# A two-layer decoder trunk on one core: the first sums of its modulation in pairs, and a new order of issue

## The chip, the cores and the metric

One core of a Trainium2 chip. Its engines work side by side: TensorE (PE, with its weight loads shown apart as PEld), VectorE (DVE), ScalarE (ACT), GpSimd (POOL) and SyncE (SP), which here only issues DMA transfers. Each engine works through its own instructions in the order in which they were issued, and waits on semaphores for the others. The metric is the device time of one execution in microseconds (us).

## The reference

A decoder trunk of two layers on x of 256 tokens by 1024 features, float32 throughout. An even layer is a combined input projection for two groups of heads (a sliding-window attention with sinks, and a sparse one with compressed, selected and window branches); an odd layer is a block-sparse attention that is a causal one at this length. What surrounds each layer is the part that this change touches:

```
c_act = silu(c)
for layer in range(2):
    ada = einsum('bd,de->be', c_act, w_ada[layer]) + b_ada[layer]
    shift, scale, gate = split(ada, 3, axis=-1)
    h = rms_norm(x, norm_g[layer]) * (1 + scale) + shift
    y = even_mixer(h, ...) if layer == 0 else odd_mixer(h, ...)
    x = x + gate * y
return rms_norm(x, final_g)
```

Layer 0 can multiply nothing by its input weights before shift and scale are there for at least a few features, and these need a matrix product of c (one row) with `w_ada`.

## The kernel before

**One list sets the order.** The whole trunk is first recorded: each call on an engine becomes a numbered operation in a `Plan`, with the operations that must come before it. Then `issue` goes through `ORDER`, a list of 3002 numbers, and issues the operations in that order. It demands only that what an operation depends on comes earlier in the list, so the list decides the order on every engine's queue, DMA issues included. All instructions carry line L244, that of the helper, so in the profile they are told apart by the names of their tiles. `group` gives a handful of operations the union of what any of them depends on, so that they stand together behind the same waits.

**The float32 products.** A large operand is split into a float32r part `hi` (a cast on ACT, tiles `whi`) and the rest `lo` (a subtraction on DVE, tiles `wlo`); the activations are split into `hhi` and `hlo`. A product is three matmuls, hi by hi, hi by lo and lo by hi, into the same bank.

**The opening.** The 1024 features are eight blocks of 128. `START` deals them out in four units: two blocks, then two, two and two. For each unit the kernel loads the columns of `w_ada` for that unit's shift and scale (1024 rows by 512 columns, 2 MB), sums them against c, turns the sums into columns (`shs`), prepares `hhi` and `hlo` of the unit's blocks, and multiplies them by the corresponding 128-row blocks of the input weights (`raw`, 128 x 1688 each, loaded in pieces of 1304 and 384 columns or finer), accumulating in the banks `ps_s`, `ps_pj`, `ps_o` and `ps_pt`. Before that come the squares of x, its scaling, and its transposes through `ps_s` and `ps_pj` into `bigA`. PE runs matmuls on `ones` in between, for which no one waits.

Unit 0's columns of `w_ada` go to four rooms: `qT_98` (shift, features 0 to 511 of c), `qT_99` (shift, 512 to 1023), `qT_100` (scale, first half) and `gate` (scale, second half, loaded in two pieces). Unit 2 uses the same rooms again; units 1 and 3 use `late`. `cz` holds silu(c) in column 0 of 32 columns, for each of eight slices k of c.

**The sums** (`start_sums`). For each of four column groups q (0 and 1 are the two blocks of shift, 2 and 3 those of scale) one row of 32 output partitions is used: the matmul has 32 stationary columns (`cz[:, k]`) at tile position 32 q and 128 moving columns. For unit 0 (d = 0) all eight k are summed on PE, 32 matmuls. For later units the first d slices are summed on DVE into `acc` and go in as one extra matmul. In the kernel before, the loops run over k outside and q inside, and groups of four matmuls are tied together. When all is summed, ACT copies the bank to `asb`, PE transposes it, DVE adds the bias and applies the norm's weight.

**The end.** After the output projection of layer 1, for each half of the tokens, DVE adds the scaled result to `xs`, sums squares, POOL takes the root, and ACT and DVE scale the columns and send them out in pieces (`LAST`): of the first half 384 columns by ACT and 640 by DVE; of the second half 192 and 192 by ACT, 256 and 384 by DVE. In the profile the scaled results are tiles `t`, and `parts` holds the sums of squares.

**Small rows.** `rows` collects norm weights, biases and the compressed branch's position terms, each a load of 16 rows of 128 (8 KB), for layer 1 and the compressed branch among them.

Of the kernel before, what the change touches and what calls it, by code (L numbers as in the profile page):

```python
# [255 lines left out]
def tile_trunk(  # L256
# [23 lines left out]
    plan = Plan(tc.nc)  # L280
# [433 lines left out]
    def start_sums(g, n, d, w):  # L714
# [29 lines left out]
        for o in range(0, len(ids), 4):  # L744
            plan.group(ids[o : o + 4])
# [640 lines left out]
```

## Time and profile before

| what | value |
|---|---|
| median of 3 runs | 295.09 us (294.73 to 295.18) |
| the profiled execution's own time | 295.04 us |
| its span, first to last instruction | 293.3 us |
| mean granted clock of TensorE | 0.995 |
| PE, DVE, ACT busy | 285.4, 252.8, 188.5 us |
| bytes moved by DMA | 71.72 MB |

The span is what the rows of the trace count from; 1.74 us of the execution's time lie around it. A busy engine is not one that works at its peak: PE's matmuls overlap and their ends are modelled. The granted clock was 1.00 in nearly all stretches, so it plays no part here. In rows of the timeline the first number is the start in us, the second the length of the group; a bracket at the end is the idle time ahead of it and what ended it. Rows of the chain of waits give start, length, and what the end of the program was waiting for at that time.

### The profile page before, as it was taken

What the parts mean: (1) busy time and instruction counts of PE and PEld (TensorE: products, weight loads), DVE (VectorE), ACT (ScalarE), POOL (GpSimd) and SP (SyncE); (2) the same over time, 40 slices, a digit from 0 to 9 for tenths busy, and PEclk for the clock granted to TensorE, in tenths of its full rate; (3) what the DMA queues carried; (4) which work ended last, traced back from release to release, by engine and by line L of the source; (5) the groups of instructions that cost most, each with busy time, mean ns of one, the idle gap of its engine ahead of it and who ended that gap; (6) DMA issues with size and microseconds to landing.
All of it is one profiled execution on the core that took longest, in us unless ns stands there. A gap on an engine that the chain in (4) does not pass through costs nothing.

```text
span 293.3 us, 6197 instructions
## 1 busy us (share of the span) xinstructions
PE 285.4 (97%) x2293; PEld 246.6 (84%) x2293; DVE 252.8 (86%) x629; ACT 188.5 (64%) x480; POOL 8.1 (3%) x33
## 2 busy tenths in 40 slices
PE   8999999999999999999999999999999999999991
PEld 8888788897897888777767899998899999887891
DVE  0497797999999999999889759779978999899884
ACT  4456256895998899994457863366658368584531
POOL 3000000000000000000020000000000000000021
PEclk9999999999999999999999999999999999999998
DMA  7999999999969942769986954569489709502003
GB/s 262 381 365 380 384 380 349 344 349 322 389 233 359 351 147 74 249 234 332 333 256 206 349 167 135 191 242 283 146 258 291 244 0 335 205 36 72 1 3 142
DMA packets 48431, 71.72 MB, mean 245 GB/s; under 512 B 2490, under 2 KB 33938, under 8 KB 48402
## 3 DMA queue, kind: packets, MB, share of 16 engines
q1 hardware_dynamic: 47906, 70.93, 70.6%
q8 instruction: 18, 0.29, 0.4%
q10 hardware_dynamic: 496, 0.41, 0.4%
q14 instruction: 11, 0.09, 0.1%
HBM read 70.28 MB, written 1.05 MB: 243 GB/s over the span
## 4 chain that ended last, share of the span: by engine, by line
PE 82%; DMA 11%; DVE 1%; ACT 1%; issue 1%; POOL 1%; POOLq 0%; DVEq 0%; ACTq 0%
PE ps_pj L244 53%; PE ps_s L244 10%; PE ps_o L244 7%; PE ps_pt L244 7%; PE ps_m L244 5%; DMA gate<-in_w_ada_dram 3%; DMA late<-in_w_ada_dram 3%; DMA raw<-in_w_in_even_dram 3%; DMA qT<-in_w_ada_dram 2%; DMA xs<-in_x_dram 1%; DVE wlo L244 1%; ACT t L244 1%; ACT whi L244 1%; POOL parts L244 1%; DVE t L244 0%
## 5 line engine op out<-in xcount | busy, mean ns | idle before, releaser
L244 ACT CAST whi<-raw 128x512 fp32r<-128x512 f32 (+2 forms) x116 | 71.8, 658 | 27.1 <-PE ps_pj L244 16.5
L244 DVE TENSOR_TENSOR wlo<-raw,whi 128x512 fp32r<-128x512 f32 (+2 forms) x100 | 71.3, 740 | 7.3 <-ACT whi L244 6.6
L244 PE MATMUL ps_pj<-hlo,whi 128*128 128x256 f32 x256 | 70.0, 288 | 0.0
L244 PE MATMUL ps_pj<-hhi,whi 128*128 128x256 f32 x256 | 69.9, 289 | 0.0
L244 PE MATMUL ps_pj<-hhi,wlo 128*128 128x256 f32 x256 | 68.3, 284 | 0.0
L244 PEld LDWEIGHTS ps_pj<-hhi,whi 128*128 128x128 f32 x256 | 46.7, 188 | 1.6 <-issue 0.7
L244 PEld LDWEIGHTS ps_pj<-hlo,whi 128*128 128x128 f32 x256 | 47.1, 189 | 0.8 <-issue 0.7
L244 PEld LDWEIGHTS ps_pj<-hhi,wlo 128*128 128x128 f32 x256 | 46.7, 189 | 0.3
L244 ACT ACTIVATE late<-late,mn 128x128 f32<-128x128 f32 (+1 forms) x58 | 26.0, 450 | 9.2 <-DVE mn L244 9.1
L244 DVE SCALAR_TENSOR_TENSOR acc<-raw,cz,acc 128x1024 f32<-128x1024 f32 x24 | 30.6, 1276 | 0.1
L244 PE MATMUL ps_pj<-whi,hlo 128*128 128x512 f32 (+2 forms) x72 | 25.6, 373 | 0.0
L244 PE MATMUL ps_pj<-wlo,hhi 128*128 128x512 f32 (+2 forms) x72 | 25.5, 372 | 0.0
L244 DVE SCALAR_TENSOR_TENSOR wlo<-raw,whi 128x512 fp32r<-128x512 f32 x32 | 21.1, 686 | 4.5 <-ACT whi L244 4.4
L244 PE MATMUL ps_pj<-whi,hhi 128*128 128x512 f32 (+2 forms) x72 | 24.8, 373 | 0.0
L244 PE MATMUL ps_pj<-wlo,ghi 128*128 128x512 f32 (+1 forms) x56 | 20.6, 371 | 0.0
L244 PE MATMUL ps_pj<-whi,ghi 128*128 128x512 f32 (+1 forms) x56 | 20.6, 371 | 0.0
L244 PE MATMUL ps_pj<-whi,glo 128*128 128x512 f32 (+1 forms) x56 | 20.4, 367 | 0.0
L244 PE MATMUL ps_pt<-ta,late 128*128 128x128 f32 x87 | 19.6, 275 | 0.0
L244 ACT COPY late<-ps_pt 128x384 f32<-128x384 f32 (+1 forms) x29 | 14.0, 483 | 7.9 <-PE ps_pt L244 7.6
L244 PEld LDWEIGHTS ps_pj<-whi,hhi 128*128 128x128 f32 x72 | 13.4, 188 | 2.5 <-ACT hhi L244 0.7
L244 PEld LDWEIGHTS ps_pj<-whi,hlo 128*128 128x128 f32 x72 | 13.6, 188 | 2.0 <-issue 0.2
L244 PEld LDWEIGHTS ps_pj<-wlo,hhi 128*128 128x128 f32 x72 | 13.4, 189 | 1.6
(243 smaller groups left out, 591.0 us busy)
## 6 DMA issues: line engine op xcount, KB each, us to landing
raw<-in_w_in_odd_dram SPq DMA_DIRECT2D x16, 1024.0 KB, 5.7
raw<-in_w_ada_dram SPq DMA_DIRECT2D x8, 1024.0 KB, 8.3
raw<-in_w_ada_dram SPq DMA_DIRECT2D x16, 512.0 KB, 6.3
raw<-in_w_in_even_dram SPq DMA_DIRECT2D x5, 1024.0 KB, 7.9
raw<-in_w_in_even_dram SPq DMA_DIRECT2D x7, 652.0 KB, 7.6
late<-in_w_ada_dram SPq DMA_DIRECT2D x16, 256.0 KB, 6.8
raw<-in_w_out_even_dram SPq DMA_DIRECT2D x4, 1024.0 KB, 5.8
raw<-in_w_out_odd_dram SPq DMA_DIRECT2D x4, 1024.0 KB, 8.7
```

The lines of the kernel that those rows point to most:

```text
L244: self.ops.append(dict(key=eng.key, deps=deps, fn=lambda: getattr(real, name)(*args, **kw)))
```

## The change

In `start_sums` the matmuls of unit 0 are recorded in pairs: first q = 0 and 1 (shift) for all k, then q = 2 and 3 (scale) for all k, and two rather than four are tied together. Units 1 to 3 are recorded as before. The second part is a new `ORDER`. The operations are the same and so is their number.

```
-        for m in range(max(len(tq) for tq in terms)):
-            for q, tq in enumerate(terms):
-                if m < len(tq):
+        size = 4 if d else 2
+        for o in range(0, 4, size):
+            for m in range(max(len(tq) for tq in terms)):
+                for q in range(o, o + size):
+                    tq = terms[q]
+                    if m >= len(tq):
+                        continue
                     ids.append(T.matmul(
...
-        for o in range(0, len(ids), 4):
-            plan.group(ids[o : o + 4])
+        for o in range(0, len(ids), size):
+            plan.group(ids[o : o + size])
...
 ORDER = [int(i) for i in """
-5 0 45 4 9 685 2 3 6 10 37 7 1 85 11 40 38 35 86 12 87 13 14 15 16 17 70 18 88 19 89 20 71 21 72 22 55 23 46 41 39 42 47
...
```

What the order of issue shows, at three places. First PE in the opening, before: the end of unit 0's sums (`ps_m`) up to the first matmul of the projection. Ahead of these rows the same alternation of shift rooms and `qT_100` or `gate` fills twelve rows.

```order
L244 MATMUL ps_m_107<-qT_99,cz 32x128 x2
L244 MATMUL ps_m_107<-gate,cz 32x128 x2
L244 MATMUL ps_m_107<-qT_99,cz 32x128 x2
L244 MATMUL ps_m_107<-gate,cz 32x128 x2
L244 MATMUL ps_s_93<-ta,t_89 128x128
L244 MATMUL ps_pj_95<-ta,t_91 128x128
L244 MATMUL ps_m_107<-ta,asb_108 128x128
L244 MATMUL ps_pj_95<-ta,t_91 128x128
L244 MATMUL ps_o_68<-ones 128x128
L244 MATMUL ps_pj_95<-ta,t_91 128x128
L244 MATMUL ps_o_68<-ones 128x128 x3
L244 MATMUL ps_s_93<-whi_110,hhi 128x512
```

In the changed kernel the shift sums on `qT_98` come right after the transposes of the first x tiles (the words to the right of the arrow are what the matmul reads):

```order
L244 MATMUL ps_o_68<-ones 128x128 x7
L244 MATMUL ps_s_92<-ta,t_89 128x128 x2
L244 MATMUL ps_m_107<-qT_98,cz 32x128 x8
L244 MATMUL ps_pt_85<-ta,rows 128x24
L244 MATMUL ps_s_92<-ta,t_89 128x128
L244 MATMUL ps_pj_94<-ta,t_91 128x128
L244 MATMUL ps_o_68<-ones 128x128
```

and the end of the sums, up to the first matmul of the projection, reads:

```order
L244 MATMUL ps_m_107<-qT_100,cz 32x128 x2
L244 MATMUL ps_s_92<-ta,t_89 128x128
L244 MATMUL ps_s_93<-ta,t_89 128x128
L244 MATMUL ps_m_107<-qT_100,cz 32x128 x2
L244 MATMUL ps_m_107<-gate,cz 32x128 x8
L244 MATMUL ps_s_93<-ta,t_89 128x128 x3
L244 MATMUL ps_pj_95<-ta,t_91 128x128 x2
L244 MATMUL ps_m_107<-ta,asb_108 128x128
L244 MATMUL ps_o_68<-ones 128x128
L244 MATMUL ps_pj_95<-ta,t_91 128x128
L244 MATMUL ps_o_68<-ones 128x128 x4
L244 MATMUL ps_s_92<-whi_110,hhi 128x512
```

All sums on the shift rooms now stand ahead of the last on `qT_100`, the eight matmuls on `gate` stand alone at the end, and five transposes of x stand between them and the transpose of the sums (`asb_108`).

Second, SP's queue in the opening, before: `raw_101` and `raw_102` are the weights of blocks 0 and 1, `late` unit 1's columns of `w_ada`.

```order
L244 DMA gate<-in_w_ada_dram 128x2x256 x2
L244 DMA raw_101<-in_w_in_even_dram 128x512
L244 DMA raw_101<-in_w_in_even_dram 128x792
L244 DMA raw_101<-in_w_in_even_dram 128x384
L244 DMA raw_102<-in_w_in_even_dram 128x1304
L244 DMA late<-in_w_ada_dram 128x2x256 x2
L244 DMA raw_102<-in_w_in_even_dram 128x384
L244 DMA late<-in_w_ada_dram 128x2x256 x6
L244 DMA raw_103<-in_w_in_even_dram 128x1304
L244 DMA raw_103<-in_w_in_even_dram 128x384
```

The same stretch now:

```order
L244 DMA gate<-in_w_ada_dram 128x2x256
L244 DMA rows<-in_b_ada_dram 16x128
L244 DMA gate<-in_w_ada_dram 128x2x256
L244 DMA raw_101<-in_w_in_even_dram 128x512
L244 DMA rows<-in_cmp_pe_v_dram 16x128
L244 DMA raw_101<-in_w_in_even_dram 128x384
L244 DMA raw_101<-in_w_in_even_dram 128x792
L244 DMA raw_102<-in_w_in_even_dram 128x384
L244 DMA qT_100<-in_w_ada_dram 128x2x256
L244 DMA raw_102<-in_w_in_even_dram 128x1304
L244 DMA late<-in_w_ada_dram 128x2x256 x5
L244 DMA rows<-in_cmp_pe_k_dram 16x128
```

Two loads of `rows` that stood far down the queue are here now (a third follows among `late`), and one of the pieces of unit 2's columns (`qT_100`, 256 KB), which stood behind `raw_104`, now precedes the 1304 columns of `raw_102`. Unit 2's other pieces follow where they did, behind `raw_104`, in another order, with both pieces for `gate` last.

Third, DVE at the end of the program, before: `t_89` takes the 640 scaled columns of the first half of the tokens, `t_88` columns of the second half, `ISA` is the sum of squares.

```order
L244 TENSOR_TENSOR xs<-xs,t_91 128x256
L244 TENSOR_TENSOR xs<-xs,bigA 128x512
L244 TENSOR_SCALAR t_89<-xs,parts 128x640
L244 TENSOR_TENSOR xs<-xs,bigA 128x256
L244 TENSOR_TENSOR xs<-xs,bigA 128x512
L244 TENSOR_TENSOR xs<-xs,ps_pj_95 128x256
L244 ISA t_90,parts<-xs,parts 128x256
L244 ISA parts 128x1
L244 TENSOR_SCALAR t_88<-xs,parts 128x384
L244 SCALAR_TENSOR_TENSOR t_88<-xs,parts,bigA 128x256
```

Now:

```order
L244 TENSOR_TENSOR xs<-xs,t_91 128x256
L244 TENSOR_TENSOR xs<-xs,bigA 128x512
L244 TENSOR_TENSOR xs<-xs,bigA 128x256
L244 TENSOR_TENSOR xs<-xs,ps_pj_95 128x256
L244 ISA t_90,parts<-xs,parts 128x256
L244 ISA parts 128x1
L244 TENSOR_SCALAR t_89<-xs,parts 128x640
L244 TENSOR_SCALAR t_88<-xs,parts 128x384
L244 SCALAR_TENSOR_TENSOR t_88<-xs,parts,bigA 128x256
```

The scaling into `t_89` stands behind the last sum of squares, ahead of the two of the second half. The order changed at many other places on all engines too, with the same operations.

231 rows, old and new, of the table ORDER are left out of this document.

## The prediction

> **What bounds the kernel now.** I read the page's busy shares first, then a table of stretches of the span, then the chain of waits. The page:
>
> ```profile
> PE 285.4 (97%) x2293; PEld 246.6 (84%) x2293; DVE 252.8 (86%) x629; ACT 188.5 (64%) x480; POOL 8.1 (3%) x33
> ```
>
> The share is an average. The table of stretches (start and end, length; then busy time and count for PE, PEld, DVE, ACT, POOL; granted clock, DMA share, GB/s) tells the stages apart:
>
> ```profile
> 0.00:15.00 15.00, 13.84 (x136) 12.85 (x137) 4.42 (x16) 6.97 (x14) 3.32 (x21) 1.00 0.92 323
> 15.00:33.00 18.00, 17.50 (x128) 14.50 (x131) 15.61 (x32) 8.98 (x20) 0.00 (x0) 1.00 1.07 373
> 33.00:52.00 19.00, 19.00 (x154) 16.21 (x153) 15.77 (x36) 10.98 (x24) 0.00 (x0) 1.00 1.05 366
> 75.00:105.00 30.00, 30.00 (x264) 25.62 (x264) 29.98 (x105) 26.87 (x86) 0.00 (x0) 1.00 0.90 320
> 167.00:240.00 73.00, 73.00 (x632) 68.54 (x632) 61.93 (x148) 40.88 (x97) 0.00 (x0) 1.00 0.62 205
> 275.00:293.30 18.30, 12.05 (x76) 10.63 (x74) 11.85 (x25) 5.46 (x13) 2.30 (x5) 0.92 0.16 59
> ```
>
> Up to 33 us the DMA engines are full; from 33 to 275 PE has no idle time; at the end PE is idle while the last rows are written. The 13.84 us of PE in the first row hold the warm-up matmuls on `ones` and other work of the opening; the first matmul of a projection comes at 14.74 (a row below). The row of 167 to 240 gives a price: 632 matmuls in 73.00 us is 0.1155 us for 256 columns, so 0.23 for 512. The chain of waits in its first 36 us (start, length, what) says which transfers set the opening:
>
> ```profile
> 0.80 3.35 DMA xs<-in_x_dram
> 4.16 7.62 DMA gate<-in_w_ada_dram
> 11.79 7.51 DMA late<-in_w_ada_dram
> 19.32 7.42 DMA raw<-in_w_in_even_dram
> 26.75 6.09 DMA qT<-in_w_ada_dram
> 32.89 1.30 PE ps_m L244 x40
> 34.19 0.67 PE ps_s L244 x2
> ```
>
> Each link is issued when an earlier transfer has landed: the second half of `gate` lands at 11.78, one transfer of `late` goes out at 11.79. Behind the last link PE takes over. So there are two barriers: the second `gate` for unit 0, and unit 2's sums at 32.89, the only place after the start where PE waited for data:
>
> ```profile
> PE ps_m L244 <- DMA qT<-in_w_ada_dram: 0.5, 1, 0.5
> ```
>
> PE reached them at 32.39. What is won ahead of 32.39 is not kept unless this barrier moves too. This is the centre of the forecast.
>
> **The change part by part.** *Unit 0's sums.* The timeline of before, DVE's row of `cz` first (start, length, what, count; one fp32 matmul on PE leaves two records):
>
> ```profile
> 9.16 0.17 DVE L244 TENSOR_SCALAR cz<-tiny 128x8 f32<-128x8 f32 x1
> 11.05 1.18 PE L244 MATMUL ps_m<-qT,cz 128*32 128x128 f32 x34
> 12.73 0.28 PE L244 MATMUL ps_m<-gate,cz 128*32 128x128 f32 x2
> 13.42 0.33 PE L244 MATMUL ps_m<-ta,asb 128*128 128x128 f32 x1
> 14.74 0.70 PE L244 MATMUL ps_s<-whi,hhi 128*128 128x512 f32 x2
> 32.89 0.64 PE L244 MATMUL ps_m<-qT,cz 128*32 128x128 f32 x16 [0.50 <-DMA qT<-in_w_ada_dram]
> 33.35 0.40 PE L244 MATMUL ps_m<-gate,cz 128*32 128x128 f32 x8
> 33.57 0.40 PE L244 MATMUL ps_m<-acc,ones 128*32 128x128 f32 x8
> 33.79 0.40 PE L244 MATMUL ps_m<-gate,cz 128*32 128x128 f32 x8
> ```
>
> A quad of four sums is 8 records and takes 33.57 - 33.35 = 0.22 us. In before all 8 quads run in one go, 11.05 to 13.01, and only then can the sums be copied and turned. Now the shift pairs, which need only `qT`, run ahead, and four pairs on `gate` are left for the end. No row shows a pair alone. From below it costs half a quad (0.11), from above a whole one (0.22), since the two columns that are missing ran beside the others; I take 0.22. In the new order three places have two pairs of different columns back to back, which I count as quads: 13 steps, 13 x 0.22 = 2.9 against 8 x 0.22 = 1.8, so 1.1 us more of PE. Nearly all of it lies in time in which PE ran `ones` and waited for landings. What counts is behind `gate`'s second half (11.78): two to four pairs, 0.44 to 0.88, so the sums end at 12.3 to 12.7 against 13.0. The earlier `cz` on DVE (the scalings of both halves of x stood ahead of it, now one does) is what lets the shift pairs go first. The first real matmul, 14.74, comes 1.7 us behind the sums by the chain copy, transpose, two small DVE operations, `hhi`, and some of the ACT casts stand beside it: I take 14.4, a gain of 0.3.
>
> The Trainium skill, TensorEngine Tiling (Array Packing), Theoretical Speedup, puts a stationary side of at most 32 at up to four times, by filling four column tiles. By it a pair wastes half the array and sixteen pairs would be 16 x 0.22 = 3.5 us; the quads of this trace, four sums in 0.22, agree with the packing, and no run here shows a pair. It changes the result only if PE and not `gate` ends the sums.
>
> *The opening's transfers.* The old queue, as SP issued it:
>
> ```profile
> 3.31 1.22 SPq L244 DMA_DIRECT2D gate<-in_w_ada_dram  x2
> 4.66 2.95 SPq L244 DMA_DIRECT2D raw<-in_w_in_even_dram  x4
> 8.79 1.89 SPq L244 DMA_DIRECT2D late<-in_w_ada_dram  x2
> 11.05 0.34 SPq L244 DMA_DIRECT2D raw<-in_w_in_even_dram  x1
> 11.79 5.90 SPq L244 DMA_DIRECT2D late<-in_w_ada_dram  x6
> 27.53 0.37 SPq L244 DMA_DIRECT2D gate<-in_w_ada_dram  x1
> ```
>
> Moved ahead: three loads of `rows` of 8 KB each and one 256 KB piece of `qT` that unit 2 needs, now in front of the 652 KB piece of `raw_102`, row block 1 of the input projection. At the 373 GB/s of the stretch 15 to 33 that is 0.7 us for the 256 KB and under 0.1 for all three small ones. So `raw_102` and unit 1's `late` come 0.7 to 0.8 later than before. The `qT` piece overwrites what the scale pairs of k = 0 and 1 read, so SP waits for PE there, with `raw_102` and all of `late` queued behind it; as PE can take those pairs before `gate` is in, I count nothing for it; if they ran last SP would go on at 12.3 instead of about 11 (it issued the other piece of `raw_102` at 11.05), and `raw_102` could come up to 1.3 later still, which B would need. PE starts on row block 1 some 3.5 us behind its first matmul (its place in the new order at the price above); I expect a stall of 0.5 to 1.0 there or at unit 1's sums, which eats the 0.3 and more. But what counts is unit 2's last `gate`: ahead of it lie 10,544 KB of SP's queue before (counted from the order) and 10,568 now, so it lands at most 0.1 later. The real matmuls ahead of unit 2's sums are the same, 15.7 us at the price above in either order. So PE arrives at 32.39 - 0.3 + (0.5 to 1.0) = 32.6 to 33.1, and waits there as before; up to about 33.2 the late arrival costs nothing, because the last 8 records on `gate` at 33.79 end the sums in any case. **Opening: between -0.5** (the barrier's whole idle time gone) **and +0.9; taken 0.**
>
> *The middle.* The same instructions in another order, under a PE that has no idle time: 0, as long as that cover holds. What an order can win or lose there are the weight loads' waits, 34 to 275 us; the largest:
>
> ```profile
> PEld ps_s L244 <- DVE mn L244: 0.8, 1, 0.8
> PEld ps_pj L244 <- ACT hhi L244: 0.7, 2, 0.4
> PEld ps_s L244 <- DVE qT L244: 0.6, 3, 0.3
> ```
>
> These three sum to 2.1 us, and as PE shows no idle time beside them at most part reached the matmuls. I bound the middle at -1.0 (half of them gone) and, by the same size, +1.0: in 75 to 105 DVE was busy 29.98 of 30.00, and a chain that moves there has nothing to hide behind. Taken -0.1, near the no-idle row.
>
> *The tail.* The scaling of 640 columns of the first half of the tokens moves on DVE from ahead of the last sums to behind them. Rows of the tail:
>
> ```profile
> 285.84 0.55 DVE L244 TENSOR_SCALAR t<-xs,parts 128x640 f32<-128x640 f32 x1
> 286.31 1.02 DVE L244 TENSOR_TENSOR xs<-xs,bigA 128x256 f32<-128x256 f32 x2
> 286.43 3.81 SPq L244 DMA_DIRECT2D out_dram<-t  x3
> 286.78 0.27 PE L244 MATMUL ps_pj<-whi,glo 128*128 128x256 f32 x1
> 287.25 0.41 DVE L244 TENSOR_TENSOR xs<-xs,ps_pj 128x256 f32<-128x256 f32 x1
> 288.38 0.55 POOL L244 TENSOR_TENSOR parts<-parts,expo 128x1 f32<-128x1 f32 x1 [1.93 <-DVE parts L244]
> 288.96 0.42 DVE L244 TENSOR_SCALAR t<-xs,parts 128x384 f32<-128x384 f32 x1 [0.67 <-POOL parts L244]
> ```
>
> PE's last matmul is over at 287.05, and DVE began on its result at 287.25, straight behind its own work: at most 0.2 to win, 0.17 taken for the handover. The moved 0.55 now lies in DVE's 0.67 of waiting for POOL, so it costs nothing while POOL takes that long. But its 320 KB of output leave at about 288.7 instead of 286.43, just ahead of the last 512 KB. At 373 GB/s they are 0.9 us; if all of that stood in the way the tail would lose 0.7, if none it would win 0.17. The last transfers go out from 289.4 on, so most is through: I take +0.1 for it, net -0.07.
>
> **Sum** against the profiled execution (span 293.3, its own time 295.04, so 1.74 around the span; the median of the runs is 295.09): 295.04 + 0 - 0.1 - 0.07 = 294.87; I say 294.9.
>
> **The rivals.** *A, faster: the order's gains are kept.* Unit 2's barrier gives back its 0.5, the tail 0.17, and 0.1 to 0.5 of the weight loads' waits goes: 295.04 - 0.8 to - 1.2 = 293.8 to 294.2. For it: the waits are real. Against: the bytes ahead of the barrier have not become fewer.
>
> *B, slower: `raw_102` behind `qT`.* The 652 KB piece lands 0.8 late, PE stalls at row block 1, unit 1's sums come 0.8 late, and both add up instead of falling together. From an arrival at unit 2 beyond 33.2 on each tenth counts; 32.09 + 1.6 = 33.7 gives +0.5, and with the blocked end of the tail (up to 0.7) +0.5 to +1.2: 295.5 to 296.2, about 295.8. For it: the DMA share of 1.07, no slack in the queue. Against: both stalls stem from one delay of 0.7.
>
> *C: small transfers are dear.* Issues wait for earlier landings (11.78, then 11.79), so a load of 8 KB takes a place in the queue like one of 256 KB. If each of the three left a hole of 0.2 the barrier would come 0.6 later: 295.5.
> The Trainium skill, DMA: Bandwidth & Descriptors, Anatomy of one DMA, gives a transfer about 2.0 us of fixed cost (a fit on the software-made kind); in series the three would be an estimated 6 us and the result 301. The chain above, with full DMA engines at seven microseconds from issue to landing, speaks against series; what one small load costs amid large ones no row of before separates.
>
> *D: it does not do what it says.* PE takes the pairs no earlier than the quads, since `cz` is not ready: then they start at 9.33, when `cz` was ready before, and 2.9 us end at 12.2, below 12.7. It falls to the same time.
>
> **How the numbers follow.** About 0.2% (0.59 us) is what a measurement of this kernel can tell from no change. The forecast, 294.5 to 295.5, has 0.47; A 0.28; B 0.15; C 0.06; D lies within the forecast with 0.04. A is faster by over 0.2% but for its edge: with the forecast's low end 0.30. B and C past 295.68: 0.19, with the middle's +1.0. Same: 0.51. The range holds A's upper part, the forecast and B's middle: 294.1 to 295.9; the forecast's own is 294.5 to 295.5.
>
> **What would show it.** Right: first real matmul at 14.3 to 14.5; a DMA wait of `raw` or `whi` at 17 to 19; unit 2's sums still ending at 34.0 to 34.3; PE's last matmul within 0.5 of 286.78; DVE on its result within 0.1 of the matmul's end. Wrong: unit 2's sums ending before 33.7 or after 34.8, or PE idle between 35 and 275.

## The result: 297.71 us against 295.01, slower by 0.9%

| what | before | changed |
|---|---|---|
| median | 295.01 us (294.73 to 295.18, 4 runs) | 297.71 us (296.75 to 297.89, 4 runs) |
| ratio | 1 | 1.0086, 95% interval 1.0063 to 1.0109 |
| the profiled execution's own time | 295.04 us | 297.89 us |
| its span | 293.3 us | 296.1 us |

The prediction was 294.9 with a range of 294.1 to 295.9: wrong in direction and outside the range. The changed kernel's page, first the busy shares and then the table of stretches (start and end, length; busy time and count of PE, PEld, DVE, ACT, POOL; granted clock, DMA share, GB/s):

```profile
PE 287.5 (97%) x2293; PEld 248.1 (84%) x2293; DVE 252.6 (85%) x629; ACT 188.6 (64%) x480; POOL 10.5 (4%) x33
```

```profile
0.00:15.00 15.00, 13.88 (x129) 12.51 (x130) 3.52 (x13) 6.03 (x12) 3.08 (x19) 1.00 0.87 297
15.00:33.00 18.00, 17.54 (x126) 14.50 (x125) 14.82 (x32) 9.95 (x22) 0.00 (x0) 1.00 1.03 345
275.00:296.10 21.10, 14.54 (x87) 12.61 (x85) 15.14 (x30) 7.11 (x16) 4.70 (x5) 0.94 0.14 50
```

PE's share is the same 97%; nothing in the first row speaks of 2.7 us. The GB/s at the end of the stretches do: 297 instead of 323 in the first 15 us, 345 instead of 373 in the next 18. Those are 0.39 and 0.50 MB that had not been moved by then. Two narrow stretches, of the changed kernel and then of the kernel before, show where most of it is missing:

```profile
13.60:16.40 2.80, 2.80 (x26) 2.51 (x23) 1.89 (x6) 2.44 (x7) 0.00 (x0) 1.00 0.62 142
```

```profile
13.60:16.40 2.80, 2.80 (x20) 2.54 (x19) 2.54 (x7) 2.80 (x7) 0.00 (x0) 1.00 1.04 379
```

142 GB/s for 2.80 us instead of 379: 0.66 MB, or 1.75 us of transfers at the old rate. There was a hole in a queue that had none before. SP's queue and its waits between 2 and 20 us tell why (rows of the timeline, then of the table of waits: us in total, times, longest):

```profile
8.00 3.35 SPq L244 DMA_DIRECT2D raw<-in_w_in_even_dram  x3
13.08 0.38 SPq L244 DMA_DIRECT2D qT<-in_w_ada_dram  x1
13.50 1.52 SPq L244 DMA_DIRECT2D raw<-in_w_in_even_dram  x1
15.06 2.87 SPq L244 DMA_DIRECT2D late<-in_w_ada_dram  x5
```

```profile
SPq L244 <- PE ps_m L244: 1.3, 1, 1.3
```

SP had issued three pieces of `raw` by 11.35 and then stood until 13.08 at the moved piece of `qT_100`. Up to then each issue had followed by some 0.02 us the landing of the transfer eight places ahead: 8.00 behind 7.99, 9.51 behind 9.49, 11.02 behind 11.00. The next such landing came at 11.75. From there to 13.08 are the 1.3 us for which the row names PE. On PE:

```profile
8.39 1.07 PE L244 MATMUL ps_m<-qT,cz 128*32 128x128 f32 x16
11.26 1.07 PE L244 MATMUL ps_m<-qT,cz 128*32 128x128 f32 x28
12.26 0.44 PE L244 MATMUL ps_s<-ta,t 128*128 128x128 f32 x2
12.62 0.41 PE L244 MATMUL ps_m<-qT,cz 128*32 128x128 f32 x4
12.87 1.04 PE L244 MATMUL ps_m<-gate,cz 128*32 128x128 f32 x16
15.70 0.70 PE L244 MATMUL ps_s<-whi,hhi 128*128 128x512 f32 x2
```

The piece overwrites what the sums of k = 2 and 3 on `qT_100` read. (The prediction wrote k = 0 and 1; the piece holds columns 512 to 1023 of the room, the third and fourth slice.) The last of these pairs stands behind two transposes of x and runs at 12.62. Behind the piece wait `raw_102` (652 KB) and all of `late`. Worked out from the landings in the trace, `raw_102` is complete at 19.11 instead of 15.52, the last `late` at 25.07 instead of 23.03, and the last `gate` of unit 2 at 35.89 instead of 33.54. The chain of waits now runs through the same places (pieces left out between):

```profile
12.69 0.37 PE ps_m L244 x4
13.06 0.02 issue
13.08 0.38 SPq L244
...
13.50 1.52 SPq L244
...
16.56 5.52 DMA late<-in_w_ada_dram
...
22.10 6.60 DMA raw<-in_w_in_even_dram
...
28.77 7.12 DMA gate<-in_w_ada_dram
...
35.93 0.43 PE ps_m L244 x8
```

PE's pair, SP's issues, then three transfers, each behind the landing of the one before, up to the end of unit 2's sums: 35.93 + 0.43 = 36.36, against 33.79 + 0.40 = 34.19. The barrier moved by 2.2 us. From there PE keeps that lag and adds little: its last matmul starts at 289.27, 2.49 behind the 286.78 of before. The end of the program, in the timeline:

```profile
289.27 0.27 PE L244 MATMUL ps_pj<-whi,glo 128*128 128x256 f32 x1
289.58 0.42 DVE L244 TENSOR_TENSOR xs<-xs,ps_pj 128x256 f32<-128x256 f32 x1 [0.36 <-PE ps_pj L244]
290.56 0.55 DVE L244 TENSOR_SCALAR t<-xs,parts 128x640 f32<-128x640 f32 x1
290.72 0.79 POOL L244 TENSOR_TENSOR parts<-parts,expo 128x1 f32<-128x1 f32 x1 [1.45 <-DVE parts L244]
291.17 1.67 SPq L244 DMA_DIRECT2D out_dram<-t  x3
291.54 0.42 DVE L244 TENSOR_SCALAR t<-xs,parts 128x384 f32<-128x384 f32 x1 [0.44 <-POOL parts L244]
```

DVE is free for PE's result: 0.31 from the last matmul's start to its own, 0.47 before. But POOL's root takes 0.79 beside the moved scaling, 0.55 before, so the last scalings start 2.27 behind PE's last matmul (2.18 before). From there to the end of the span are 4.56 us (4.34 before), with 320 KB more ahead of the last output. Together 0.31 later. So of the span's 2.8 us 2.17 arise up to the end of unit 2's sums, 0.32 between there and PE's last matmul, and 0.31 behind it.

### The profile page after: what moved, and what is told of

The parts are those of the page before. It is cut to its first block, busy times and chain, and to the rows that moved or that the text cites. A ratio compares the mean times of both kernels' runs of the same rounds, so it can differ in the third digit from the quotient of the medians.

```text
span 296.1 us, 6176 instructions
## 1 busy us (share of the span) xinstructions
PE 287.5 (97%) x2293; PEld 248.1 (84%) x2293; DVE 252.6 (85%) x629; ACT 188.6 (64%) x480; POOL 10.5 (4%) x33
## 4 chain that ended last, share of the span: by engine, by line
PE 86%; DMA 6%; DVE 2%; SPq 1%; issue 1%; POOL 0%; POOLq 0%; ACT 0%; DVEq 0%; ACTq 0%
PE ps_pj L244 55%; PE ps_o L244 10%; PE ps_s L244 8%; PE ps_pt L244 7%; PE ps_m L244 6%; DMA gate<-in_w_ada_dram 2%; DMA raw<-in_w_in_even_dram 2%; DMA late<-in_w_ada_dram 2%; DVE t L244 1%; SPq L244 1%; DVE xs L244 1%; POOL parts L244 0%; POOLq L1385 0%; ACT t L244 0%; DVEq L1385 0%
## 5 line engine op out<-in xcount | busy, mean ns | idle before, releaser
L244 PE MATMUL ps_pj<-whi,hhi 128*128 128x512 f32 (+2 forms) x72 | 26.3, 372 | 0.0
L244 PE MATMUL ps_pt<-ta,late 128*128 128x128 f32 x87 | 19.0, 274 | 0.0
L244 ACT COPY asb<-ps_m 128x128 f32<-128x128 f32 (+1 forms) x7 | 2.2, 312 | 19.8 <-PE ps_m L244 19.8
```

Source lines behind the costliest of these rows:

```text
L244: self.ops.append(dict(key=eng.key, deps=deps, fn=lambda: getattr(real, name)(*args, **kw)))
```

## The experiments

In the diffs the numbers are operations in `ORDER`: 216 is the moved piece of `qT_100` (columns 512 to 1023), 215 the other, 211 the first piece of `qT_98`, 101 the 1304 columns of `raw_102`, 102 its 384, 93 to 100 `late`, 526, 528 and 529 small loads of `rows`, 2936 DVE's scaling of 640 columns and 2937 its output. Each median stands beside the kernel before in the same batch, on one chip. The changed kernel itself had medians of 297.71, 296.48 and 297.72 in three batches, so where figures of two batches are put together, the text says so. The ratios go by means and can differ from the quotient of the medians. A profile shows one execution, and where a kernel's runs scatter it can lie well above the median. In some of the kernels the helper stands in line L249.

### First batch: one part of the change undone or done alone

**The `qT` piece back** (changed kernel, 216 to its old neighbours):

```
-... 132 133 216 134 79 ...  248 252 215 193 ...
+... 132 133 134 79 ...  248 252 216 215 193 ...
```

> The changed kernel with one transfer moved: the 256 KB piece of qT for unit 2 goes back behind raw_104, next to the other piece of qT_100. Theory H (a hole in the transfers: SP stood before that piece from 11.4 to 13.07 waiting for PE's last pair on qT_100, and the DMA engines ran dry behind it): SP no longer waits, raw_102's 1304 columns land at 16 to 17.5 instead of 19.1, unit 2's last gate at 33.6 to 34.3 instead of 35.9, and the time falls by 1.5 to 2.3, to 295.4 to 296.2. Theory S (the small loads of rows leave holes) and theory M (the new order behind 36 us is what is slow): at most 0.5 less, 297.2 or more.

Measured: 296.23 us against 295.02 (ratio 1.0041, 1.0029 to 1.0053). SP goes on to `raw_102` at once, and unit 2's sums end at 34.44, 0.25 behind before:

```profile
11.01 1.07 SPq L249 DMA_DIRECT2D raw<-in_w_in_even_dram  x2
34.04 0.40 PE L249 MATMUL ps_m<-gate,cz 128*32 128x128 f32 x8
```

H had given 295.4 to 296.2. The hole comes with the piece. 1.2 us stay, which it does not explain.

**The piece ahead of `raw_102` in the kernel before** (101 and two of `late` follow it):

```
-... 62 52 101 63 ... 67 95 103 ... 112 98 113 ... 117 118 119 ... 199 216 254 ...
+... 62 52 63 ... 67 103 ... 112 113 ... 117 118 216 101 95 98 119 ... 199 254 ...
```

> The kernel before with the opposite move alone: the same 256 KB piece of qT ahead of raw_102's 1304 columns, quads as they were. Theory H: SP waits for the last quad on qT_100, at about 12.0, raw_102 lands 1.5 to 3 later than 15.5, the last gate of unit 2 0.6 to 1.8 later than 33.5, and the time rises by 0.6 to 1.8, to 295.6 to 296.8. Theory S and theory M: no change, within 0.3 of 295.0, since the bytes ahead of the barrier stay the same.

Measured: 296.00 us against 295.02 (1.0046, 1.0027 to 1.0065): about 1.0 slower with this move, within H's 0.6 to 1.8; the three loads had to go behind the piece with it. In the profile (297.16, well above the median) SP waits there too (`SPq <- PE ps_m` 1.1 us), and the sums of unit 2 end 1.8 later:

```profile
12.44 0.38 SPq L249 DMA_DIRECT2D qT<-in_w_ada_dram  x1
35.62 0.40 PE L249 MATMUL ps_m<-gate,cz 128*32 128x128 f32 x8
```

**The three small loads of `rows` back** (rival C of the prediction):

```
-... 88 526 56 ... 23 529 24 ... 149 528 171 ... 409 421 530 ...
+... 88 56 ... 23 24 ... 149 171 ... 409 421 529 528 526 530 ...
```

> The changed kernel with its three small loads of rows (8 KB each) moved back to where they stood, ahead of srow's load. Theory S: 0.6 or more less, 297.1 or below. Theory H: SP's wait at the piece of qT is the same, so at most 0.3 less, 297.4 to 297.9.

Measured: 296.99 us against 295.02 (1.0066, 1.0045 to 1.0086), and the wait is there as before: `qT` goes out at 13.24, with 1.7 us of waiting for PE. The small loads are not the cause of the hole. What they are worth in time is not settled: 296.99 lies below the 297.1 that S had named, but the changed kernel was not in this batch, and its own medians reach from 296.48 to 297.72.

**The tail back** (changed kernel, scaling and output of the 640 columns ahead of the last sums):

```
-... 2963 2978 ... 2992 2936 2993 2937 3000 ...
+... 2963 2936 2937 2978 ... 2992 2993 3000 ...
```

> The changed kernel with DVE's scaling of 640 columns and its output moved back ahead of the last sums. The prediction's reading (0.17 won at the hand-over, about 0.1 lost to the output): 0.1 slower than the changed kernel, 297.8. Theory P (the scaling lies beside POOL's root, which took 0.79 instead of 0.55, and its 320 KB leave just ahead of the rest): 0.2 to 0.4 faster, 297.3 to 297.5, with POOL's root at 0.55 again.

Measured: 296.22 us against 295.02 (1.0047, 1.0026 to 1.0068), with single runs from 295.67 to 298.64. POOL's root takes 0.55 again. Neither 297.8 nor 297.3 to 297.5 came. The changed kernel was not in this batch and its runs scatter, so the tail's price is not read from here but from the run of the tail in the kernel before, below.

### Second batch: queues exchanged, the tail alone

**The changed kernel again**, with nothing altered, so that the others have it beside them.

> The changed kernel again, beside the three that follow, since its four runs reached from 296.75 to 297.89. All theories: 296.7 to 297.9; the profile's hole in front of raw_102 shows again (SP held until about 13, last gate of unit 2 at 35.5 to 36.5).

Measured: 296.48 us (295.88 to 297.57) against 295.01 (1.0057, 1.0041 to 1.0072). The median is a little under the 296.7 expected. The scatter of the changed kernel is part of the result: in its profiled execution here, 297.33 us, SP issues the piece at 12.64.

**The changed kernel's work with the whole SP queue of before, and the reverse.** The places of SP's operations in `ORDER` stay as they are, and filled with them in the other kernel's sequence:

```
-SP: 88 526 89 90 529 92 91 102 216 101 96 94 93 ...
+SP: 88 89 90 91 92 101 95 98 102 93 94 97 96 ...
```

> The changed kernel's order on PE, DVE, ACT and POOL with the old queue of SP, whole. Theory H (the loss sits in the order of the transfers): 295.0 to 295.8, with unit 2's sums ending at 34.0 to 34.5; what is left over 295.0 is the tail (POOL's root beside DVE's scaling) and the new middle. Theory M (the new order of the computing engines loses it): 296.5 or more.

> The other half: the order of before on PE, DVE, ACT and POOL, quads in it, with the new queue of SP. Theory H: 296.0 to 297.3, a hole in front of raw_102 as in the changed kernel, since SP waits for the last quad on qT_100. Theory M: 295.0 to 295.4.

Measured: 299.70 us (1.0167, 1.0152 to 1.0182) and 300.62 us (1.0173, 1.0140 to 1.0205) against 295.01. Both are worse than either kernel. With the old queue the hole is gone, but the halves of x arrive in the other order than the work expects and the first projection matmul starts at 16.35. Queue and work are fitted to each other, and exchanging a whole queue says nothing about one transfer in it. M's "296.5 or more" came true by its letter, its 295.0 to 295.4 for the reverse did not, and neither of H's two ranges did. Neither theory is decided by this pair.

**The tail's move alone, in the kernel before:**

```
-... 2965 2982 2936 2983 ... 2987 2937 2988 ... 2992 2993 2996 2994 3000 ...
+... 2965 2982 2983 ... 2987 2988 ... 2992 2936 2993 2996 2994 2937 3000 ...
```

> The kernel before with DVE's scaling of 640 columns and its output moved behind the last sum of squares, nothing else. Theory P: 0.2 to 0.5 slower, 295.2 to 295.5, with POOL's root at 0.79 instead of 0.55 and the last operations 0.1 to 0.3 later behind PE's last matmul. The prediction's reading: 0.07 faster, 294.9.

Measured: 295.46 us (295.21 to 295.59) against 295.01 (1.0013, 1.0005 to 1.0022): the move costs 0.45. Its timeline has the parts in small:

```profile
286.85 0.27 PE L249 MATMUL ps_pj<-whi,glo 128*128 128x256 f32 x1
287.16 0.42 DVE L249 TENSOR_TENSOR xs<-xs,ps_pj 128x256 f32<-128x256 f32 x1
288.30 0.79 POOL L249 TENSOR_TENSOR parts<-parts,expo 128x1 f32<-128x1 f32 x1 [1.68 <-DVE parts L249]
```

DVE 0.31 behind PE (0.16 won), the root 0.79 (0.24 lost), and 4.58 instead of 4.34 us from the last scalings' start, 289.12, to the end of the span of 293.7. That makes 0.32 in this profile; the medians say 0.45.

### Third batch: what about the piece costs time, and what is left

**Another piece in its place:** 216 and 211 exchanged. Bytes and queue stay the same, but the readers of `qT_98`'s first piece are done by 9.5 in the changed kernel.

```
-... 132 133 216 134 ... 197 186 211 224 ...
+... 132 133 211 134 ... 197 186 216 224 ...
```

> The changed kernel with two transfers of 256 KB exchanged: ahead of raw_102's 1304 columns now goes unit 2's first piece of qT_98, whose old contents PE had read by 9.4, and the piece of qT_100 takes its place behind raw_104. The bytes ahead of raw_102 and ahead of the barrier are the same as in the changed kernel; only what SP waits for differs. Theory H (SP's wait for PE's last pair on qT_100 is what costs): as with the piece moved back, 295.6 to 296.4, SP past this place by 12, raw_102's 1304 columns landed at 17 to 18. Theory B (256 KB more ahead of raw_102 are what costs): as the changed kernel, 296.5 to 297.7.

Measured: 296.26 us against 295.17 (1.0041, 1.0026 to 1.0057). By the medians that is 1.09 above before, beside 1.21 (first batch) and 0.86 (fourth) for the kernel with the piece back, and 2.70, 1.47 and 2.65 for the changed kernel in its three batches. So it stands with the kernel that has no piece there, and inside H's 295.6 to 296.4, as if what the piece waits for cost more than its bytes do. The changed kernel was not beside it in this batch, so this speaks for the wait without settling it. The profiled execution (297.27, one of two above 297 among six) is not clean. Two rows of SP's waits between 2 and 20 us:

```profile
SPq L249 <- DMA gate<-in_w_ada_dram: 0.5, 1, 0.5
SPq L249 <- PE ps_m L249: 0.2, 1, 0.2
```

The piece goes out at 12.57, only 0.08 behind the landing of the transfer eight places ahead, a piece of `gate`, at 12.49. So here SP stood for a place in the queue and next to nothing for PE (the event behind the second row comes at 12.75, when the issue has begun). Unit 2's sums still end at 35.80, 1.6 behind before: an execution can lose that much without a wait for PE at this place.

**The last pair on `qT_100` ahead of the two transposes:**

```
-... 123 124 63 65 64 125 126 127 ...
+... 123 124 125 126 63 65 64 127 ...
```

> The changed kernel with one pair of matmuls moved: the last pair on qT_100 runs ahead of two transposes of x instead of behind them, so SP is let go 0.3 to 0.4 earlier, at 12.6 to 12.8. Theory H: 0.1 to 0.4 faster than the changed kernel (296.5 to 297.7 so far), a shorter hole. Otherwise the same.

Measured: 296.42 us against 295.17 (1.0052, 1.0039 to 1.0064). Whether this is 0.1 to 0.4 under the changed kernel, as expected, cannot be told, since that one was not in the batch. In its profile (295.96 us, the lowest of five runs) the piece goes out at 11.95, 1.1 earlier, and unit 2's sums end at 34.53 instead of 36.36:

```profile
11.95 0.38 SPq L249 DMA_DIRECT2D qT<-in_w_ada_dram  x1
34.10 0.43 PE L249 MATMUL ps_m<-gate,cz 128*32 128x128 f32 x8
```

The wait does follow PE's pair: PE is through with the last of them at 11.87. About 0.5 of the 1.1 is not the move's, since this run of pairs already starts at 10.77 instead of 11.26. SP still waits 0.6 us for PE. The median stays above this profile's own time; what the other executions lose was not profiled.

**The piece and the tail back together** (the edits of the first batch combined):

> The changed kernel with the piece of qT and the scaling of 640 columns both moved back. If the two add: 0.45 (the tail moved alone in before) under the 296.23 of the piece alone, 295.6 to 295.9. What is then left over 295.0 is the rest of the new order (the opening's other moves and the middle). If the two do not add: 296.2 as either alone.

Measured: 295.58 us against 295.17 (1.0013, 1.0003 to 1.0023). 0.41 is left (0.1 to 0.7 by the interval) that neither the piece nor the tail explains.

**ACT takes the 640 columns, in the kernel before:**

```
-LAST = ((("a", 0, 384), ("v", 384, 1024)), ...
+LAST = ((("a", 0, 384), ("a", 384, 1024)), ...
```

> The kernel before with the 640 columns of the first half scaled by ACT instead of DVE (the table LAST, nothing else); ACT was idle from 286.0 to 288.96. If DVE's own work was what held up its start on PE's last result (287.25, PE done at 287.05) and POOL's root is not disturbed by ACT: 0.1 to 0.2 faster, 294.8 to 294.9. If the hand-over costs the same anyway: 295.0.

Measured: 294.93 us against 295.17 (0.9991, 0.9982 to 1.0000). DVE is free at once and POOL's root keeps its 0.55:

```profile
285.87 0.81 ACT L244 ACTIVATE t<-xs,parts 128x640 f32<-128x640 f32 x1
287.01 0.42 DVE L244 TENSOR_TENSOR xs<-xs,ps_pj 128x256 f32<-128x256 f32 x1
288.15 0.55 POOL L244 TENSOR_TENSOR parts<-parts,expo 128x1 f32<-128x1 f32 x1 [1.69 <-DVE parts L244]
```

What the tail's move meant to win (DVE 0.31 instead of 0.47 behind PE) is to be had by moving the scaling to another engine instead of to a later place. It is the lowest median of all kernels here, 0.24 below before, though the interval touches 1.

### Fourth batch: the sizes, all beside the changed kernel

> The changed kernel once more, so that the three kernels beside it can be compared with it on one chip. Both theories: 296.3 to 297.7 against about 295.05 for the kernel before (the medians so far were 296.48 and 297.71).

> The changed kernel with the moved qT piece back in its old place, beside the changed kernel on one chip. Theory H (the hole in the transfers, from SP waiting at that piece, costs the larger part): at least 0.7 below the changed kernel of this batch. Rival (the hole is covered in most executions, and only its profiled one shows it): within 0.3 of it.

**The old opening under the new rest:** the first 400 operations as in before (the pairs kept), all later ones as in the changed kernel.

```
-ORDER = (the changed kernel's)
+ORDER = (first 400 of before's) + (the others in the changed kernel's order)
```

> The pairs kept, the first 400 operations in the order of before (with unit 0's shift pairs in the first eight places of its sums and the scale pairs in the last eight), all later ones in the order of the changed kernel. Theory: the opening accounts for all but the tail (0.45) and 0.2 of the middle, so 295.05 + 0.65 = 295.7. Rival: the rest of the order is worse than that by itself, and this stays at 296.2 or more.

**The pairs alone, in the kernel before** (`start_sums` as changed; unit 0's eight shift pairs in the first eight places of its sums, the scale pairs in the last eight):

> The kernel before with the pairs alone: unit 0's eight shift pairs take the first eight places of its sums and the scale pairs the last eight; nothing else is moved. The sums should then end 0.25 to 0.4 earlier than 13.01, since only four pairs of 0.24 stay behind the second half of gate. Theory: unit 2's sums wait for the same transfers, so the time stays within 0.2 of before. Rival (what is won in the opening is kept): 0.3 faster.

| kernel | median (us) | runs | ratio, 95% interval |
|---|---|---|---|
| before | 295.07 | 20 | 1 |
| changed | 297.72 (295.90 to 298.39) | 6 | 1.0076 (1.0053 to 1.0100) |
| changed, `qT` piece back | 295.93 (295.81 to 296.87) | 5 | 1.0033 (1.0021 to 1.0044) |
| changed, old opening | 295.88 (295.67 to 296.35) | 8 | 1.0029 (1.0019 to 1.0039) |
| before with the pairs alone | 295.08 (294.77 to 295.49) | 11 | 0.9997 (0.9988 to 1.0007) |

By the medians the one piece is worth 297.72 - 295.93 = 1.79 us, where H had given at least 0.7 and its rival at most 0.3, and the whole opening 297.72 - 295.88 = 1.84: the piece is all of it but 0.05. These sizes are loose, because the changed kernel's six runs spread over 2.5 us: by the ratios, which go by means, the piece is worth 0.43%, or 1.3 us, and the opening 0.47%, or 1.4. That 1.79 lies so near to the 1.75 us read from the hole is luck. In this batch's profile of the changed kernel (297.37) the same narrow stretch ran at 298 GB/s, not 142, and unit 2's sums ended 1.63 later than before; with the piece back (296.87, the highest of its five) they ended 0.57 later.

Of the 0.81 that stay with the old opening (0.65 had been expected), 0.45 are the tail, measured in the second batch; 0.36 lie in the order between the opening and the tail. With the piece and the tail back these sizes give 0.36 + 0.05 = 0.41, and 0.41 was measured in the third batch.

The pairs alone change nothing, and how they do that is the most instructive row of the study. PE's opening in that kernel:

```profile
10.49 2.41 PE L249 MATMUL ps_m<-qT,cz 128*32 128x128 f32 x48
12.73 1.04 PE L249 MATMUL ps_m<-gate,cz 128*32 128x128 f32 x16
15.46 0.70 PE L249 MATMUL ps_s<-whi,hhi 128*128 128x512 f32 x2
33.88 0.40 PE L249 MATMUL ps_m<-gate,cz 128*32 128x128 f32 x8
```

My expectation that the sums would end 0.25 to 0.4 earlier was wrong. Sixteen pairs take from 10.49 to 13.77, 0.20 each, where eight quads took 11.05 to 13.01; they end 0.8 later, the first projection matmul starts at 15.46 instead of 14.74, and at unit 2's sums nearly all of it is gone: they end at 34.28, 0.09 behind before. The slack ahead of that barrier swallowed a loss of 0.7. It swallows a gain too: in the profile of the run in which ACT takes the 640 columns, with the opening of before, the first projection matmul came at 14.33, 0.41 earlier, and unit 2's sums ended at 34.19 all the same.

With the old opening unit 2's sums end at 34.07, 0.12 earlier than before, but PE's last matmul starts at 287.24, 0.46 later (the table of waits shows no idle time of PE between 33 and 115 us). From the end of unit 2's sums to PE's last matmul it takes 253.17 us there, 252.91 in the changed kernel's first profile and 252.59 before, so the traces too put a few tenths into this part. Which of the moved operations in between costs the 0.36 was not taken apart.

## Why the prediction was wrong

**The step that failed** is in *The opening's transfers*: the wait of the moved `qT` piece for PE, "I count nothing for it", because PE could take those pairs before `gate` is in. In this order it did not: the last of them stands behind two transposes of x, none of them starts before 11.26, and SP waited 1.3 us for PE. (With the last pair ahead of the transposes PE was through at 11.87, and the second half of `gate` landed at 12.20.) I had seen this possibility ("if they ran last SP would go on at 12.3 instead of about 11") and put it into rival B. The printed order, quoted ahead of the prediction, shows the last pair on `qT_100` just ahead of the eight on `gate`: the row that decided was there, and I argued from what PE could do.

**The second half of that step**, "it lands at most 0.1 later", was worked out from bytes ahead of the barrier, 10,544 KB and 10,568 KB. That holds only while the queue never stands still. It stood for 1.3 us, and with the long issue of `raw_102` behind it (1.52) the DMA engines ran at 142 instead of 379 GB/s for 2.8 us. The last `gate` landed 2.34 later, and the opening cost 1.84 by the medians (1.4 by the means, 2.17 in that profile) where 0 was taken and +0.9 was its upper bound.

**Rival B** named the mechanism, with 0.15, and its price, 295.5 to 296.2, was also too small. It counted `raw_102` as 0.8, at most 0.8 + 1.3, late; it came 3.6 late. What it priced was one transfer behind another, not a whole queue behind a wait. That the wait itself was the 1.3 that B needed is in part luck: both of its ends, 11.75 and 13.06, came 0.7 to 0.8 later than written.

**The pairs' price** was right: the four pairs on `gate`, from 12.87 to 13.91, start 0.22 apart, as taken. Their place was wrong: the sums end at 13.91, not at 12.3 to 12.7, since twelve pairs, not four, stand behind 11.26. The first projection matmul came at 15.70, not 14.4. By itself this did not cost the 2.7 us: the pairs alone made the first matmul 0.7 late and the time did not change. The Trainium skill, TensorEngine Tiling (Array Packing), Theoretical Speedup, lets a stationary side of 32 win up to four times only by filling four column tiles; the run of the pairs alone agrees in direction (0.20 a pair, 0.24 a quad, so half the sums in nearly the same time). I had written that this matters only if PE and not `gate` ends the sums; PE did end them, and in the run of the pairs alone it still did not matter.

**The barrier at unit 2** as the place at which the opening's gains and losses are settled was right, in both directions: 0.7 lost ahead of it cost nothing (pairs alone), and the 2.2 lost at it in the changed kernel's profile are still there at PE's last matmul (2.49).

**Rival C**, dear small loads, fell as the cause of the hole: with the three back in their old places the wait was there as before (1.7 us). Their own price was not measured beside the changed kernel. **Rival A** and **rival D** did not occur, though D's "PE takes the pairs no earlier" was nearly true of the scale pairs.

**The middle**, -0.1 with bounds of -1.0 and +1.0: +0.36 by the old opening under the new rest. Inside the bounds, on the other side.

**The tail**, -0.07 with bounds of -0.17 and +0.7: +0.45 alone in the kernel before. The win at the handover was right (0.17 predicted, 0.16 measured). Two terms were mis-sized. "It costs nothing while POOL takes that long" took POOL's 0.55 as fixed, but the moved scaling itself made it 0.79. And the output of the 640 columns cost 0.22 in the profile, where 0.1 was taken.

The sum, by the medians of the fourth batch and the tail of the second: 295.07 + 1.84 + 0.36 + 0.45 = 297.72. It must come out, since the middle in it is what the other terms leave; the run with the piece and the tail both back is the check on it that was not used to make it. By the first profile the three parts are 2.17, 0.32 and 0.31.

## What to carry to other kernels

In a queue that issues in order, a load that is moved ahead is priced by what it waits for (the readers of the room that it overwrites, at their place in the new order), and then by everything queued behind it; bytes ahead of a barrier tell its time only while the queue cannot stand still. Work that is moved into another engine's waiting time has to be looked at for what it does to that engine, because the cover can grow with it. And ahead of a barrier set by transfers, a change in the compute work alone shows nothing, good or bad, within the slack there (here 0.7 lost and 0.4 won).

## What was not expected of the hardware

**The changed kernel scatters.** Its sixteen executions reach from 295.88 to 298.39 us. The lowest, 295.88 and 295.90, are as low as the same kernel with the piece back, which suggests that nothing of the hole is left in some; none of those was profiled. Two things differ between the profiled ones. SP's issue of the 652 KB of `raw_102` took 1.52, 1.61 and 1.35 us in three profiles with the wait (two of the changed kernel, one with the small loads back) and 0.47 in a third of the changed kernel. But there the issue behind it, of `late`, took 1.18, and with the piece back, without the wait, one of `late` took 1.53: one long issue between 13 and 15.5 us is in each of these profiles, whichever load stands there, and its cause is open.

And the sixteen parts of one transfer spread out: the first 512 KB of `qT` had its first and last landing at 6.71 and 7.99 in the changed kernel, at 6.72 and 7.26 before, and at 6.65 and 8.04 with the piece back (fourth batch). Since places in the queue come free with the last landing, the issues behind it come later too. The spread was 0.54 to 0.82 in the six profiles with the whole queue of before and 0.84 to 2.39 in those with the new one or one changed in a place, but also 1.47 with the piece ahead of `raw_102` in the kernel before, whose queue is the old one up to there. Why it opens stays open, and so does how much of the wait of 1.3 us, in which `qT_100` was complete at 11.00 instead of 10.28, is due to it.

**GpSimd beside VectorE.** The root on one column took 0.55 us alone and 0.79 beside the scaling of 640 columns, in all eleven profiles with that order, and 0.55 in all seven with the scaling elsewhere. The Trainium skill, SBUF — State Buffer, Who interferes with whom, has the two engines share a port pair, with one fully blocked while the other holds it, for scalings in a two-port mode. The trace agrees in sign: the two overlap by 0.39 us (290.72 to 291.11), and 0.24 of it is lost. That the port is the cause was not tested.
